# Pairwise products of an RWKV-7 layer: two 64-row products, each head in its half of the array, in place of one 128-row product with zero-filled columns

## The chip, the core and the metric

The kernel runs on one core of a Trainium2 chip. The metric is the device time of one execution in microseconds; the time before is the median of three runs. The profile is of a single execution, taken by the hardware profiler.

## What is computed

The model is a two-layer trunk on 1024 positions of width 1024. Layer 0 is a latent attention (MLA) mixer, layer 1 an RWKV-7 mixer; each has four heads of attention to a memory of 256 rows, a SiLU gate and an output projection. The change lies in layer 1, whose 24 heads of width 64 carry a state through this recurrence:

```
def step(state, inp):
    r_t, w_t, k_t, v_t, kk_t, a_t = inp
    sa = einsum('bhvk,bhk->bhv', state, -kk_t)
    state = (state * w_t[:, :, None, :]
             + sa[..., None] * (kk_t * a_t)[:, :, None, :]
             + v_t[..., None] * k_t[:, :, None, :])
    return state, einsum('bhvk,bhk->bhv', state, r_t)
```

The kernel does not step through positions. It cuts the sequence into chunks of 64 positions. Within a chunk, the products of all pairs of positions (the decayed keys against the decayed queries, one 64x64 block for each kind of pair) are made at once by a matrix multiplication and masked to the causal triangle; a triangular system is inverted, and only the state between chunks is carried in order.

## The kernel before

All work is float32. The large projections split each operand into a rounded part and a remainder and add three products (`mm3`, L160 to L162), with weights streamed from memory, rounded on ScalarE (L152) and subtracted on VectorE (L153). Other products take plain float32; each of those stands twice in the trace, as two weight loads and two passes of the moving operand.

Layer 1 works on 24 *items*: 12 pairs of heads, each for the first and then the second half of the sequence. A tile of 128 partitions holds one pair, head 0 in rows 0 to 63 and head 1 in rows 64 to 127. An item goes through five stages, `project`, `prep`, `invert`, `scan` and `norm`. In each step of the outer loop five successive items are in the five stages, and generators give their code in turn (`interleave`). The framework then places the instructions on each engine when the program is built, so the order on an engine is neither that of one stage nor quite that of the generators. Each engine executes its instructions in that order.

The change is in `prep`. An item there has eight chunks `c`, and these names:

- `BK[i][:, j, :]`, 128 partitions x 128: for a chunk, 64 columns of one kind of key and 64 of the other. It is the stationary operand.
- `AR[:, c, :]`, 128 partitions x 256: four blocks of 64 columns, two kinds (`j`) for head 0 and head 1 (`h`). The rows of head 0 are filled only in the blocks of head 0, and the rows of head 1 only in those of head 1 (L1050, L1051); the rest is zero. It is the moving operand, and the scan uses it too (L1214, L1224).
- `a_tile()`: a tile of one PSUM bank, from a pool of two. The same pool serves other products of `prep`, the memory heads and a norm.
- `AM[i]`: the masked products of two chunks, 128 x 2 x 256, read by the scan (L1212, L1225), by the DMAs to `sysd` (L1103) and by ScalarE (L1106). `am` is the mask.

Before, each chunk is one product (L1085) over all 128 rows with all 256 columns: the zeros keep the two heads apart. Two chunks fill a bank, and one VectorE multiplication by the mask (L1087) moves the bank to `AM[i]`. That is eight products, four banks and four multiplications for an item.

Two other places of layer 1 matter to the argument. `invert` has four products over 32 rows alone for each item (L1171), and eight transposes into 32 columns (L1148). The scan is a chain through the chunks: L1212 and L1214 into a bank, `gm` (L1216), L1218, `SAV` (L1219), L1221, the new state (L1233).

Of the kernel before, what the change touches and what calls it, by code (L numbers as in the profile page):

```python
# [18 lines left out]
ALU = mybir.AluOpType  # L19
# [4 lines left out]
P = 128  # L24
# [47 lines left out]
class Build:  # L72
# [903 lines left out]
    def prep(self, d, env):  # L976

        p, r, k, v, AR = (d[x] for x in ("p", "r", "k", "v", "AR"))
        twa = d["twa"]
        rmask, am, a_tile = (env[x] for x in ("rmask", "am", "a_tile"))  # L980
        nc = self.nc
        mm = nc.tensor.matmul
        V, G, ACT = nc.vector, nc.gpsimd, nc.scalar
# [7 lines left out]
        for j, (t, bias) in enumerate(((sig, PW0), (a, PA0))):  # L991
            ps = a_tile()
# [8 lines left out]
        ps = a_tile()  # L1001
# [6 lines left out]
        ps = a_tile()  # L1008
# [19 lines left out]
        f = self.smp.tile([P, 16], F32, tag="f", name=self.name("f"))  # L1028
# [9 lines left out]
        ps = a_tile()  # L1038
# [5 lines left out]
        BK = [self.g([P, 4, P], s="BK") for _ in range(2)]  # L1044
        SAV, BKT, AM = [], [], []
        V.tensor_mul(Dx[:], kk[:], Dx[:])
        V.tensor_mul(L[:], r[:], L[:])
        for hd in range(2):
            rows, c0 = slice(hd * 64, hd * 64 + 64), hd * 64
# [10 lines left out]
        ps = a_tile()  # L1060
# [9 lines left out]
        for i in range(2):  # L1070
            yield
            ps = a_tile()
# [4 lines left out]

        yield

        for i in range(4):  # L1080
            yield
            ps = a_tile()
            for j in range(2):
                c = 2 * i + j
                mm(ps[:, j * 256 : j * 256 + 256], BK[c // 4][:, c % 4, :], AR[:, c, :], start=True, stop=True)  # L1085
            AM.append(self.g([P, 2, 256], s="AM"))
            V.tensor_tensor(  # L1087
                out=AM[i][:], in0=ps[:].rearrange("p (c f) -> p c f", f=256),
                in1=am.unsqueeze(1).broadcast_to([P, 2, 256]), op=ALU.mult,
            )  # L1090

        yield

# [282 lines left out]
```

## Time and profile before

| | |
|---|---|
| three runs | 2515.22, 2519.84, 2521.16 us; median 2519.84 |
| the profiled execution | 2510.56 us, its span 2508.8 us |
| TensorE busy (PE) | 2420.2 us, 96% |
| VectorE busy (DVE) | 1936.4 us, 77% |
| ScalarE busy (ACT) | 1375.7 us, 55% |
| mean granted TensorE clock | 0.996 |
| layer 1's items, products L1085 | from 1043.8 to 2351.3 us |

PE rows are matrix passes, PEld rows the loads of their weights; a load normally runs beside the pass ahead of it. A pass is pipelined and its printed duration contains that pipeline, so the printed durations of neighbours overlap: how much array time a pass takes is read from start to start. A row of the timeline has the start, the duration, the engine, the line, the operation, the tiles (output<-inputs), then rows*columns of the array that are in use, the moving operand, and how many instructions of that kind follow one another. "32*128" is thus a weight tile over 32 rows of the array.

### The profile page before, as it was taken

How to read it: one execution, taken by the hardware profiler on the slowest of the kernel's cores; microseconds unless marked ns; L12 is line 12 of the kernel's file. 1: busy time of each engine (PE TensorE's matmuls, PEld its weight loads, DVE VectorE, ACT ScalarE, POOL GpSimd, SP SyncE). 2: the span in 40 equal slices, each digit the busy share in tenths (PEclk: the TensorE clock that was granted, in tenths of full speed). 3: DMA queues.
4: the chain of work that ended last, by engine and by line, in shares of the span. 5: the costliest groups of instructions: out<-in, count | busy, mean ns of one | idle time of the engine just before them, and what ended most of it. 6: DMA issues, size and time to landing. Idle time of an engine off the chain costs nothing.

```text
span 2508.8 us, 39875 instructions
## 1 busy us (share of the span) xinstructions
PE 2420.2 (96%) x13298; PEld 1996.1 (80%) x13298; DVE 1936.4 (77%) x5750; ACT 1375.7 (55%) x2973; POOL 55.1 (2%) x158
## 2 busy tenths in 40 slices
PE   8899999999999999999999999999999999999997
PEld 6698888888888778877778777777777777788785
DVE  7756455877787766698888888888888898786975
ACT  6445345554555334565665666666666665654542
POOL 0000000000000100000000000000000000000000
PEclk9999999999999999999999999999999999999998
DMA  5352222111112443422122222322222123222332
GB/s 178 111 171 85 76 80 74 51 56 54 49 64 68 159 168 136 143 78 76 58 73 79 80 79 78 100 82 77 79 81 80 62 84 118 87 94 98 118 137 70
DMA packets 165982, 231.45 MB, mean 92 GB/s; under 512 B 46096, under 2 KB 67984, under 8 KB 165776
## 3 DMA queue, kind: packets, MB, share of 16 engines
q1 hardware_dynamic: 165776, 228.90, 27.7%
q8 instruction: 105, 1.72, 0.3%
q14 instruction: 101, 0.83, 0.1%
HBM read 187.66 MB, written 37.49 MB: 90 GB/s over the span
## 4 chain that ended last, share of the span: by engine, by line
PE 75%; DVE 15%; ACT 6%; issue 3%; DMA 2%; SPq 0%; DVEq 0%; ACTq 0%
PE mm L160 15%; PE mm L161 15%; PE mm L162 15%; PE a L1085 3%; PE c L1218 2%; DVE tmp L1136 2%; PE pt L724 2%; DVE U L1140 2%; PE c L1221 1%; PE y L1225 1%; PE po L160 1%; PE po L161 1%; PE y L1224 1%; DVE wl L153 1%; PE po L162 1%
## 5 line engine op out<-in xcount | busy, mean ns | idle before, releaser
L152 ACT CAST wh<-wr 128x512 fp32r<-128x512 f32 (+3 forms) x500 | 299.0, 600 | 436.0 <-PE mm L161 381.0
L153 DVE TENSOR_TENSOR wl<-wr,wh 128x512 fp32r<-128x512 f32 (+3 forms) x500 | 329.6, 661 | 132.3 <-ACT wh L152 113.0
L160 PE MATMUL mm<-xnh,wh 128*128 128x512 f32 x912 | 373.9, 410 | 0.8 <-DVE qml L134 0.6
L161 PE MATMUL mm<-xnl,wh 128*128 128x512 f32 x912 | 371.2, 407 | 0.0
L162 PE MATMUL mm<-xnh,wl 128*128 128x512 f32 x912 | 369.7, 406 | 0.0
L160 PE MATMUL mm<-yh,wh 128*128 128x512 f32 x492 | 198.9, 404 | 4.3 <-DVE xr L389 4.1
L162 PE MATMUL mm<-yh,wl 128*128 128x512 f32 x492 | 196.8, 400 | 0.0
L160 PEld LDWEIGHTS mm<-xnh,wh 128*128 128x128 f32 x912 | 172.1, 189 | 30.5 <-issue 2.6
L161 PE MATMUL mm<-yl,wh 128*128 128x512 f32 x492 | 195.5, 397 | 0.0
L161 PEld LDWEIGHTS mm<-xnl,wh 128*128 128x128 f32 x912 | 172.3, 189 | 27.2 <-issue 1.4
L162 PEld LDWEIGHTS mm<-xnh,wl 128*128 128x128 f32 x912 | 172.1, 189 | 27.3 <-issue 1.0
L160 PE MATMUL mm<-xh,wh 128*128 128x512 f32 x416 | 165.2, 398 | 7.6 <-ACT xh L438 7.6
L161 PE MATMUL mm<-xl,wh 128*128 128x512 f32 x416 | 164.9, 396 | 0.6 <-DVE xl L439 0.6
L1140 DVE TENSOR_TENSOR U<-U,tmp 128x60 f32<-128x60 f32 (+24 forms) x744 | 155.9, 210 | 12.3 <-PE b L1171 0.5
L1136 DVE TENSOR_TENSOR tmp<-As,U 128x60 f32<-128x60 f32 (+24 forms) x744 | 155.6, 209 | 12.1
L162 PE MATMUL mm<-xh,wl 128*128 128x512 f32 x416 | 164.3, 395 | 0.0
L1232 ACT ACTIVATE sc<-S,f 128x128 f32<-128x128 f32 x168 | 67.4, 401 | 169.5 <-DVE S L1233 155.9
L302 ACT ACTIVATE p<-b,sm 128x512 f32<-128x512 f32 (+2 forms) x144 | 82.8, 579 | 107.3 <-DVE sm L299 82.2
L389 DVE TENSOR_TENSOR xr<-mm,xr 128x512 f32<-128x512 f32 x123 | 84.5, 688 | 67.1 <-PE mm L162 65.2
L160 PEld LDWEIGHTS mm<-yh,wh 128*128 128x128 f32 x492 | 92.7, 188 | 22.6 <-DVE xr L389 3.5
L297 DVE TENSOR_REDUCE sm<-b 128x1 f32<-128x256 f32 (+1 forms) x176 | 90.3, 527 | 24.8 <-PE b L686 10.1
L162 PEld LDWEIGHTS mm<-yh,wl 128*128 128x128 f32 x492 | 92.7, 188 | 17.0 <-issue 0.2
(361 smaller groups left out, 5968.8 us busy)
## 6 DMA issues: line engine op xcount, KB each, us to landing
wr<-in_wu_dram SPq DMA_DIRECT2D x292, 256.0 KB, 2.7
wr<-in_wo_dram SPq DMA_DIRECT2D x122, 256.0 KB, 2.6
yr<-y SPq DMA_DIRECT2D x60, 256.0 KB, 3.8
As<-sysd SPq DMA_DIRECT2D x24, 512.0 KB, 4.3
y<-y SPq DMA_DIRECT2D x32, 256.0 KB, 2.0
y<-sg SPq DMA_DIRECT2D x32, 256.0 KB, 2.0
g<-u SPq DMA_DIRECT2D x24, 256.0 KB, 2.3
gt<-g SPq DMA_DIRECT2D x24, 256.0 KB, 2.8
```

The costliest lines, as they stand in the source:

```text
L152: nc.scalar.copy(hi[:, :n], raw[:, :n])
L153: nc.vector.tensor_sub(lo[:, :n], raw[:, :n], hi[:, :n].bitcast(F32))
L160: mm(ps, a[0], b[0], start=start, stop=False)
L161: mm(ps, a[0], b[1], start=False, stop=False)
L162: mm(ps, a[1], b[0], start=False, stop=stop)
L297: nc.vector.tensor_reduce(sm[:, i : i + 1], ps[:, :own], AX.X, ALU.max, negate=True)
L302: nc.scalar.activation(p[:, :own], ps[:, :own], AF.Exp, bias=sm[:, 0:1], accum_out=sm[:, 2 + i : 3 + i])
L389: nc.vector.tensor_add(xs[m][:], ps[:], xs[m][:])
L1085: mm(ps[:, j * 256 : j * 256 + 256], BK[c // 4][:, c % 4, :], AR[:, c, :], start=True, stop=True)
L1136: E.tensor_tensor(out=tmp[:, 0:u, 0:n], in0=As[:, 0:u, u : u + 1].broadcast_to([P, u, n]), in1=U[:, u : u + 1, i0:8].broadcast_to([P, u, n ...
L1140: E.tensor_tensor(out=U[:, 0:u, i0:8], in0=U[:, 0:u, i0:8], in1=tmp[:, 0:u, 0:n], op=ALU.add)
L1232: ACT.activation(sc[:], cur, AF.Copy, scale=fc)
```

## The change

Each chunk becomes two products, one for each head. A product takes the head's 64 rows of `BK` and `AR` alone, and of `AR` only that head's two blocks of 64 columns, so that 128 columns move and no zeros. The two heads use different halves of the array's rows and write into two banks, four chunks to a bank. The bank pair is then multiplied by the mask in four pieces, each of two chunks and one head, into the same places of `AM` as before.

```
-        for i in range(4):
+        by_head = lambda t, hd: t.rearrange("p (j h t) -> p j h t", j=2, h=2)[:, :, hd, :]
+        for g in range(2):
             yield
-            ps = a_tile()
-            for j in range(2):
-                c = 2 * i + j
-                mm(ps[:, j * 256 : j * 256 + 256], BK[c // 4][:, c % 4, :], AR[:, c, :], start=True, stop=True)
-            AM.append(self.g([P, 2, 256], s="AM"))
-            V.tensor_tensor(
-                out=AM[i][:], in0=ps[:].rearrange("p (c f) -> p c f", f=256),
-                in1=am.unsqueeze(1).broadcast_to([P, 2, 256]), op=ALU.mult,
-            )
+
+            pss = [a_tile(), a_tile()]
+            for j in range(4):
+                for hd in range(2):
+                    rows = slice(hd * 64, hd * 64 + 64)
+                    mm(
+                        pss[hd][:, j * P : j * P + P].rearrange("p (j t) -> p j t", j=2), BK[g][rows, j, :],
+                        by_head(AR[rows, 4 * g + j, :], hd), start=True, stop=True,
+                    )
+            yield
+            for i in range(2):
+                AM.append(self.g([P, 2, 256], s="AM"))
+                for hd in range(2):
+                    V.tensor_tensor(
+                        out=AM[-1][:].rearrange("p c (j h t) -> p c j h t", j=2, h=2)[:, :, :, hd, :],
+                        in0=pss[hd][:, i * 256 : i * 256 + 256].rearrange("p (c j t) -> p c j t", c=2, j=2),
+                        in1=by_head(am, hd).unsqueeze(1).broadcast_to([P, 2, 2, 64]), op=ALU.mult,
+                    )
```

Lines behind this place have numbers higher by ten: L1212 becomes L1222. The new products are L1088, the new multiplications L1096.

On TensorE, the first group of chunks of the third item stood like this before (`a` is the bank; between the products stand pieces of the scan of an earlier item):

```order
L1085 MATMUL a_12173<-AR_10127,BK_12011 128x256
L1221 MATMUL c_12052<-SAV_11120,BKT_11157 128x128
L1225 MATMUL y_11918<-SAV_11120,AM_11263 128x128
L1085 MATMUL a_12173<-AR_10127,BK_12011 128x256
L1085 MATMUL a_12178<-AR_10127,BK_12011 128x256
L1212 MATMUL c_12081<-SAV_11120,AM_11263 128x128
L1214 MATMUL c_12081<-S_2585_11916,AR_10125 128x128
L1224 MATMUL y_11918<-S_2585_11916,AR_10125 128x128
L1085 MATMUL a_12178<-AR_10127,BK_12011 128x256
L1218 MATMUL c_12086<-gm_12084,XT_10128 128x128
```

All of these use the array's 128 rows. Now the same place of TensorE's order reads as follows, where `a_12197` is the bank of head 0 (rows 0 to 63) and `a_12198` that of head 1 (rows 64 to 127):

```order
L1088 MATMUL a_12197<-AR_10127,BK_12035 128x128 x2
L1231 MATMUL c_12076<-SAV_11120,BKT_11157 128x128
L1235 MATMUL y_11942<-SAV_11120,AM_11268 128x128
L1088 MATMUL a_12198<-AR_10127,BK_12035 128x128 x2
L1088 MATMUL a_12197<-AR_10127,BK_12035 128x128
L1088 MATMUL a_12198<-AR_10127,BK_12035 128x128
L1222 MATMUL c_12105<-SAV_11120,AM_11268 128x128
L1224 MATMUL c_12105<-S_2585_11940,AR_10125 128x128
L1234 MATMUL y_11942<-S_2585_11940,AR_10125 128x128
L1088 MATMUL a_12197<-AR_10127,BK_12035 128x128
L1088 MATMUL a_12198<-AR_10127,BK_12035 128x128
L1228 MATMUL c_12110<-gm_12108,XT_10128 128x128
```

Four products of 256 columns became eight of 128, in three blocks with 128-row products ahead of and behind each. Over the whole program there are 384 products L1088 in 128 such blocks: 16 blocks have one product, 46 two, 29 three, 19 four, 11 five or six, 7 eight.

On VectorE, the multiplications by the mask of that group stood among the steps of the inversion (`tmp`, `U`) and of the scan like this:

```order
L1087 TENSOR_TENSOR AM_12176<-a_12173,cst 128x512
L1136 TENSOR_TENSOR tmp_11829<-As_11826,U_11828 128x12x5
L1216 TENSOR_TENSOR gm_12161<-c_12158,cst 128x128
L1140 TENSOR_TENSOR U_11828<-U_11828,tmp_11829 128x12x5
L1087 TENSOR_TENSOR AM_12181<-a_12178,cst 128x512
```

Now there are four, each of half the width, and the last one that reads a bank stands ten rows behind the first:

```order
L1096 TENSOR_TENSOR AM_12207<-a_12197,cst 128x4x64
L1146 TENSOR_TENSOR tmp_11853<-As_11850,U_11852 128x12x5
L1096 TENSOR_TENSOR AM_12207<-a_12198,cst 128x4x64
L1150 TENSOR_TENSOR U_11852<-U_11852,tmp_11853 128x12x5
L1226 TENSOR_TENSOR gm_12185<-c_12182,cst 128x128
L1146 TENSOR_TENSOR tmp_11853<-As_11850,U_11852 128x11x6
L1096 TENSOR_TENSOR AM_12210<-a_12197,cst 128x4x64
L1150 TENSOR_TENSOR U_11852<-U_11852,tmp_11853 128x11x6
L1229 COPY SAV_11124<-c_12187 64x128
L1146 TENSOR_TENSOR tmp_11853<-As_11850,U_11852 128x10x6
L1096 TENSOR_TENSOR AM_12210<-a_12198,cst 128x4x64
```

The bank of head 0 is free after the third, that of head 1 after the fourth. The rest of the program keeps its instructions; some of them stand a few places earlier or later.

## The prediction

> **What bounds the kernel.** I read the page first, for the shares of the span and the chain that ended last. Its rows are the busy time and share of each engine, and the chain's shares by engine.
>
> ```profile
> span 2508.8 us, 39875 instructions
> ...
> PE 2420.2 (96%) x13298; PEld 1996.1 (80%) x13298; DVE 1936.4 (77%) x5750; ACT 1375.7 (55%) x2973; POOL 55.1 (2%) x158
> ...
> PE 75%; DVE 15%; ACT 6%; issue 3%; DMA 2%; SPq 0%; DVEq 0%; ACTq 0%
> ```
>
> TensorE is the bound. Next I read the stretch in which the changed products lie, 1040 to 2360 us, as one window, and the chain by line for that stretch.
>
> ```profile
> 1040.00:2360.00 1320.00, 1280.79 (x7098) 1040.32 (x7097) 1114.80 (x3866) 814.74 (x1784) 22.84 (x44) 1.00 0.26 83
> by line: PE mm L160 11.5%; PE mm L162 11.1%; PE mm L161 11.1%; PE a L1085 6.0%; DVE tmp L1136 3.1%; issue 3.0%; DVE U L1140 2.9%; PE c L1218 2.8%; PE c L1221 2.6%; PE y L1225 2.3%; PE y L1224 2.1%; PE c L1212 2.0%; PE c L1214 1.9%; ACT yT L
> ```
>
> After the length come PE, PEld, DVE and ACT busy. In this stretch PE is busy for 1280.8 of 1320 us and DVE for 84%, at the full granted clock (1.00). The products L1085 alone are 6.0% of the chain there, 79 us. Array time given or taken at this place therefore shows almost fully in the end.
>
> **The products.** What they take now is read from the groups by form (the count, then busy time and mean) and from start to start in the timeline.
>
> ```profile
> L1085 PE MATMUL a<-AR,BK 128*128 128x256 f32 x384 | 101.6, 382 | 0.0
> L1087 DVE TENSOR_TENSOR AM<-a,cst 128x512 f32<-128x512 f32 x96 | 65.2, 681 | 1.8 <-PE a L1085 0.8 <-PE y L1224 0.4
> L738 DVE TENSOR_TENSOR y<-po,gt 128x256 f32<-128x256 f32 x48 | 20.1, 419 | 3.3 <-PE po L162 3.1
> ...
> 1434.08 1.46 PE L1085 MATMUL a<-AR,BK 128*128 128x256 f32 x6
> ...
> 1438.51 0.38 PE L1212 MATMUL c<-SAV,AM 128*128 128x128 f32 x2
> 1438.73 0.39 PE L1214 MATMUL c<-S,AR 128*128 128x128 f32 x2
> ```
>
> Six passes L1085 last 1.46 us and one 0.38, so a pass of 256 columns takes (1.46 - 0.38) / 5 = 0.216 us. Two passes of 128 columns take 0.22 (1438.51 to 1438.73), 0.110 each. The 384 passes are 82.9 us, and nearly all of it was the 79 us of the chain.
>
> The change makes 768 passes of 128 columns from them. If the halves of the array take turns, that is 768 x 0.110 = 84.5 us: nothing is gained, because the zeros that are left out were columns, and the columns of the two heads add up to as many. Only if a pass of head 0 runs beside one of head 1 is there a gain. How much depends on the order: I let a pass start beside the one ahead of it only when that one is in the other half, and not before it. Going block by block through the built order, a block of two alternating products then takes three slots for its four passes, and the 128 blocks take 576 slots, 63.4 us. No row of this trace shows two halves at work together. The ends are therefore 63.4 and 84.5; no row is nearer to either, and I take the middle, 74.0: 8.9 us less than now.
>
> **The switch of the array's rows.** The kernel already has products over fewer rows, L1171 over 32. The PE timeline at two of these places, and the weight loads at the first:
>
> ```profile
> 1399.93 0.39 PE L162 MATMUL mm<-mpth,mvs 128*128 128x512 f32 x1
> 1400.16 0.40 PE L993 MATMUL a<-twa,w2h 128*128 128x512 f32 x1
> 1400.48 1.15 PE L1171 MATMUL b<-X,inv 32*128 32x128 f32 x8
> 1401.57 0.51 PE L994 MATMUL a<-twa,w2l 128*128 128x512 f32 x1
> 1401.91 0.39 PE L993 MATMUL a<-twa,w2h 128*128 128x512 f32 x1
> ...
> 1668.12 0.39 PE L162 MATMUL mm<-xnh,wl 128*128 128x512 f32 x1
> 1668.44 1.15 PE L1171 MATMUL b<-X,inv 32*128 32x128 f32 x8
> 1669.52 0.50 PE L160 MATMUL mm<-xnh,wh 128*128 128x512 f32 x1
> 1669.86 0.40 PE L161 MATMUL mm<-xnl,wh 128*128 128x512 f32 x1
> ...
> 1399.93 0.19 PEld L993 LDWEIGHTS a<-twa,w2h 128*128 128x128 f32 x1
> 1400.48 0.96 PEld L1171 LDWEIGHTS b<-X,inv 32*128 32x128 f32 x8 [0.36 <-DVE U L1140]
> 1401.57 0.19 PEld L994 LDWEIGHTS a<-twa,w2l 128*128 128x128 f32 x1
> 1401.67 0.19 PEld L993 LDWEIGHTS a<-twa,w2h 128*128 128x128 f32 x1
> ```
>
> A load usually starts with the pass ahead of its own: that of L993 starts at 1399.93, its pass at 1400.16. The first load of L1171 does not: it starts at 1400.48, together with its own pass and 0.32 us after the start of L993, whose array time is only 0.23. The same happens on leaving: the load of L994 starts with its pass at 1401.57. From L993 at 1400.16 to the second 512-column pass behind it at 1401.91 are 1.75 us, and the array time in between is 0.23 + 8 x 0.11 + 0.23 = 1.34. The block costs 0.41 us beyond its passes. The second place gives 1669.86 - 1668.12 - 1.34 = 0.40. The waiting row names VectorE's `U` as releaser on the way in; on the way out there is no such name, and both ways are as long, so I read this as the price of the switch itself, 0.20 each way: the array empties, then a load stands bare. Fewer columns, in contrast, cost nothing:
>
> ```profile
> 1447.33 0.39 PE L162 MATMUL mm<-xnh,wl 128*128 128x512 f32 x1
> 1447.55 0.60 PE L1148 MATMUL b<-cst,U 128*32 128x128 f32 x4
> 1447.99 0.39 PE L1212 MATMUL c<-SAV,AM 128*128 128x128 f32 x2
> ```
>
> Four passes into 32 columns take 0.44 us from start to start with no gap on either side. The change puts 64-row products into 128 blocks, each with 128-row products on both sides, and before it had none: 128 x 0.40 = 51.2 us on TensorE. The ends are 0 (the L1148 row, a narrow tile that costs nothing) and 51.2 (the L1171 rows, where rows are fewer, as here); I take the nearer, 51.2.
>
> The Trainium skill, "TensorEngine Tiling (Array Packing)", section Tiling Modes, says of this that "Changing tiling mode (not just tile) drains the TensorE". It speaks against the change: by it a switch to 64 rows must drain as the 32-row blocks do in this trace, and going from one half to the other inside a block must not. Its next point, that tiles load weights and multiply in parallel, would put the products at 63.4 us and the sum of both terms at +31.7 instead of +42.3; no run here shows that part yet.
>
> **VectorE.** 96 multiplications of 512 columns (65.2 us) become 192 of 256 from a bank; L738 is such an operation, at 0.419. That is 80.4 us, 15.2 more. VectorE has 16% free in this stretch and is 15% of the page's chain, so I put 0.15 x 15.2 = 2.3 us on the path; the ends are 0 and 15.2.
>
> **The banks.** Both banks of the pool are now taken together, and the second group's first product waits for the third multiplication of the first. Before, this wait was small, in the answer on L1085:
>
> ```profile
> its engine sat idle before it (us, times) until:
>   ACT BKT L1076: 1.3, 7
>   DVE AM L1087: 0.5, 2
> ```
>
> Its cover is the projection and scan products that stand between the groups, in the third item 17 of them, about 3 us, against 4 x 0.419 = 1.7 us of multiplications. I take 1 us for the program; the ends are 0 and, if that cover is gone for all 24 items, 24 x 1.7 = 40. ScalarE's copies, the DMAs of `AM` and the scan's reads are the same in number and bytes; the copies and DMAs feed the inversion one step later and have a step's time as cover.
>
> **The sum.** TensorE: 51.2 - 8.9 = +42.3 us. Between 0.75 (PE's share of the whole chain) and 0.95 (79 of L1085's 82.9) reach the end; some blocks stand where TensorE waits for the scan anyway, and I take 0.9: +38.1. With 2.3 and 1.0 it is +41.4. The profiled execution took 2510.56 us and would take 2552; it lies 9.3 us under the median of the three runs, and on the median, 2519.84, the forecast is 2561 us, 1.6% slower. About 0.3%, 7.6 us, is what a measurement of this kernel can tell from no change.
>
> **The rivals.** (a) *Faster: the halves overlap and the switch to 64 rows is free*, as for L1148. Then TensorE has 63.4 - 82.9 = -19.5; with 0.9 and the 3.3 of the other terms that is -14, 2506 us. It decides if a block's switch costs less than about 0.12 us ((19.5 x 0.9 - 3.3) / (128 x 0.9)). Against it stand the L1171 rows. Chance 0.10. (b) *It does nothing for the array*: no overlap, free switch, 84.5 - 82.9 = +1.6, with the rest +5: 2525 us. Chance 0.07. (c) *VectorE binds*: all 15.2 us fall on the path, +54, 2574 us. For it speaks its 84% in the stretch; against it, that slower products leave it more room. Chance 0.06. (d) *The banks bind*: TensorE stands before the second group in most items; with half of the 40 us it is +60, 2580 us, with all +80. The 0.5 us of now and the 17 products between speak against it. Chance 0.07.
>
> **How the numbers follow.** My forecast, the switch paid, has 0.70. Its own range goes from overlap at the low share of the chain, 31.7 x 0.75 + 3.3 = +27, to turns at the high share, 52.8 x 0.95 + 3.3 = +53: 2547 to 2573 us. The range of 8 in 10 reaches from 2522, which takes in (b), to 2585, which takes in (c) and the first half of (d); it leaves out (a) and the rest of (d). Faster by over 0.3% is (a), 0.10; within 0.3% is (b), 0.07; slower is the rest, 0.83.
>
> **What the next profile would show.** The switch: the first load of an L1088 block starting with its own pass, and 0.40 us more than the passes from the 128-row pass ahead to the second one behind. The overlap: passes L1088 of the two banks starting in pairs, a block of eight products taking about 1.0 us (9 x 0.110) rather than 1.8 (16 x 0.110). The multiplications: 0.42 us each. The banks: L1088 waiting for AM for more than a few us. I am wrong if a block of 64-row products follows a 128-row pass without a gap; then the time is below 2530. I am also wrong if going from one half to the other drains too, which would show as 0.2 us between passes and put the time above 2590.

## The result

The changed kernel takes 2531.35 us (median of four runs, 2530.25 to 2533.18) against 2517.66 for the kernel before (four runs, 2515.22 to 2521.16). The ratio is 1.0051, with a 95% interval of 1.0035 to 1.0067: 13 us slower by the ratio, where 41 were forecast. The direction was right, the size three times too large; the time lies below the 2547 to 2573 us that the forecast gave for its own mechanism.

The page of the profile after, the rows that answer to those of before:

```profile
span 2531.3 us, 40731 instructions
...
PE 2448.4 (97%) x13682; PEld 2004.6 (79%) x13682; DVE 1942.1 (77%) x5846; ACT 1374.6 (54%) x2973; POOL 55.4 (2%) x158
...
PE 76%; DVE 13%; ACT 6%; issue 2%; DMA 2%; SPq 0%; DVEq 0%; ACTq 0%
```

The groups of the new products and multiplications, with their idle time and what ended it:

```profile
L1088 PE MATMUL a<-AR,BK 64*128 64x128 f32 x768 | 91.0, 302 | 0.0
L1096 DVE TENSOR_TENSOR AM<-a,cst 128x256 f32<-128x256 f32 x192 | 76.9, 418 | 7.7 <-PE a L1088 6.8
L1088 PEld LDWEIGHTS a<-AR,BK 64*128 64x128 f32 x768 | 66.3, 187 | 21.0 <-issue 4.1 <-ACT BKT L1076 1.5 <-DVE SAV L1229 1.5
```

TensorE is still the bound and is 28 us busier. The multiplications cost what L738 said (0.418). TensorE's loads do not wait for the multiplications: among all the releasers of L1088, of which the row shows three, AM does not appear. The timeline of TensorE at the first block, eight products and so sixteen passes:

```profile
1046.56 0.39 PE L162 MATMUL mm<-yh,wl 128*128 128x512 f32 x1
1046.88 1.16 PE L1088 MATMUL a<-AR,BK 64*128 64x128 f32 x16
1047.97 0.50 PE L160 MATMUL mm<-yh,wh 128*128 128x512 f32 x1
1048.31 0.39 PE L161 MATMUL mm<-yl,wh 128*128 128x512 f32 x1
```

From 1046.56 to 1048.31 are 1.75 us. The two 512-column passes take 0.23 each, the switch 0.39 in all, and 0.90 is left for sixteen passes that would take 1.79 in turn: they run in eight pairs. The trace's starts of single passes show it: the first two are 6 ns apart, then 0.207 us pass with the bare loads, then a pair starts every 0.112 us. Two smaller blocks, in the scan of the third item:

```profile
1126.57 0.93 PE L1088 MATMUL a<-AR,BK 64*128 64x128 f32 x8
1127.43 0.49 PE L1222 MATMUL c<-SAV,AM 128*128 128x128 f32 x2
1127.76 0.39 PE L1224 MATMUL c<-S,AR 128*128 128x128 f32 x2
1127.98 0.39 PE L1234 MATMUL y<-S,AR 128*128 128x128 f32 x2
1128.30 0.49 PE L1088 MATMUL a<-AR,BK 64*128 64x128 f32 x4
1128.72 0.49 PE L1228 MATMUL c<-gm,XT 128*128 128x128 f32 x2
```

The block at 1128.30 has two products. From L1234 at 1127.98 to L1228 at 1128.72 are 0.74 us; two passes L1234 take 0.22 of it, and the first pass of L1228 still waits for its bare load. Over all 128 blocks the medians are 0.195 us for the way in, 0.193 for the way out, and for the passes 0.23 (blocks of two products), 0.45 to 0.46 (three and four) and 0.90 (eight). (14 of the 46 blocks of two start no pair and take 0.45; the order shown ahead of the prediction has such a block, with both products in one bank and so in one half.) Over 128 rows, two products take 0.45, four 0.89 and eight 1.79. So with 0.39 for the switch a block of two loses, one of four breaks even, and only long ones gain; 91 of the 128 blocks have three products or fewer.

One sum serves below. For each block I take the time from the start of the pass ahead to the start of the second pass behind, less the array time of those two, and add up the blocks; waits inside are contained, those of the first product too. Before, this is 87 us, after, 112: TensorE spends 25 us more. Each such sum is from one profiled execution, each time and ratio from several.

### The profile page after: what moved, and what is told of

Its sections match the earlier page's. It is cut to its first block, busy times and chain, and to the rows that moved or that the text cites. A ratio compares the mean times of both kernels' runs of the same rounds, so it can differ in the third digit from the quotient of the medians.

```text
span 2531.3 us, 40731 instructions
## 1 busy us (share of the span) xinstructions
PE 2448.4 (97%) x13682; PEld 2004.6 (79%) x13682; DVE 1942.1 (77%) x5846; ACT 1374.6 (54%) x2973; POOL 55.4 (2%) x158
## 4 chain that ended last, share of the span: by engine, by line
PE 76%; DVE 13%; ACT 6%; issue 2%; DMA 2%; SPq 0%; DVEq 0%; ACTq 0%
PE mm L160 16%; PE mm L162 15%; PE mm L161 15%; PE a L1088 3%; PE c L1228 2%; PE c L1231 2%; PE pt L724 2%; PE y L1235 1%; PE c L1222 1%; DVE wl L153 1%; PE po L160 1%; PE po L161 1%; DVE tmp L1146 1%; PE y L1234 1%; DVE U L1150 1%
```

## The experiments

The theory: the switches cost TensorE 0.39 us a block, the overlap gives passes back, and most of either reaches the end. The rival: TensorE's part is absorbed by waits, and the loss comes from the narrow multiplications and from holding both banks.

### No switch and no overlap: the heads apart, over 128 rows

The two operands of `mm` change, the rest of the call (`...`) stays:

```
-  ... BK[g][rows, j, :],
-  by_head(AR[rows, 4 * g + j, :], hd), ...
+  ... BK[g][:, j, :],
+  by_head(AR[:, 4 * g + j, :], hd), ...
```

> The products of the changed kernel, one for each head into its own bank, but over all 128 rows (the other head's rows are zero in these columns): no row switch and no overlap, while the bank pairs and the eight narrow multiplications on VectorE stay. Theory (the loss is the 128 row switches on TensorE, about 0.39 us each, against a gain from the overlap): TensorE has 768 passes of 0.110 = 84.5 us instead of 82.9, so the time is that of the kernel before plus 1 to 5 us, ratio 1.000 to 1.002. Rival (the switches are absorbed by waits, and the loss comes from VectorE's narrow multiplications and from holding both banks): the same loss as the changed kernel or more, plus 10 to 16 us, ratio 1.004 to 1.006.

Measured: 2515.5 against 2518.3 us, ratio 0.9989 (0.9979 to 0.9998). The kernel stands in exactly the changed kernel's order on TensorE, VectorE and ScalarE, with the same multiplications and banks, and it is 3 us faster than the kernel before, not 10 to 16 slower. The rival falls. The theory's plus 1 to 5 us is missed too, a little on the other side: TensorE's blocks take 93 us, 6 more than before, so the narrow multiplications, the banks and the new order together cost nothing here.

### The switch without the overlap: both heads on one half

```
-  ... BK[g][rows, j, :],
-  by_head(AR[rows, 4 * g + j, :], hd), ...
+  ... BK[g][0:64, j, :],
+  by_head(AR[0:64, 4 * g + j, :], hd), ...
```

This kernel leaves out head 1's products: rows 0 to 63 hold zeros in the columns of head 1.

> The changed kernel with both heads' products put on rows 0 to 63, so that head 1's products use the rows of head 0 and its masked products come out as zeros; on every engine the instructions stand in exactly the order of the changed kernel. All 128 blocks switch, and no pass has a partner in the other half. Theory (switches cost TensorE 0.39 us each block, overlap gives back 28.7 us of passes, some eight tenths of either reach the end): TensorE has about 141 us in these blocks against 112 in the changed kernel, so 20 to 27 us slower than it and 34 to 40 slower than before, ratio 1.013 to 1.016. Rival (what TensorE saves or loses here is mostly absorbed by waits of the scan): within 8 us of the changed kernel, ratio 1.004 to 1.008.

Measured: ratio 1.0162 (1.0146 to 1.0179), 2560.0 us, 41 slower than before and 28 slower than the change; the theory's upper ends were 40 and 27. With it there are three kernels of the same order on these engines. Their first block, first in this kernel, then in the one over 128 rows:

```profile
1047.82 0.39 PE L162 MATMUL mm<-yh,wl 128*128 128x512 f32 x1
1048.14 2.05 PE L1088 MATMUL a<-AR,BK 64*128 64x128 f32 x16
1050.12 0.50 PE L160 MATMUL mm<-yh,wh 128*128 128x512 f32 x1
1050.45 0.39 PE L161 MATMUL mm<-yl,wh 128*128 128x512 f32 x1
```

```profile
1049.99 0.39 PE L162 MATMUL mm<-yh,wl 128*128 128x512 f32 x1
1050.22 1.95 PE L1088 MATMUL a<-AR,BK 128*128 128x128 f32 x16
1051.92 0.48 PE L160 MATMUL mm<-yh,wh 128*128 128x512 f32 x1
1052.23 0.40 PE L161 MATMUL mm<-yl,wh 128*128 128x512 f32 x1
```

Between the 512-column passes at the ends lie 2.63 us on one half (1047.82 to 1050.45), 2.24 over 128 rows, and 1.75 with both halves. The switch is the 0.39 between the first two, the overlap the 0.88 between the first and the last. In the whole program:

| | TensorE in the blocks | ratio to before | against the row above |
|---|---|---|---|
| over 128 rows | 93 us | 0.9989 | |
| one half: switch alone | 137 us | 1.0162 | +44 us for +44 on TensorE |
| both halves: switch and overlap (the change) | 112 us | 1.0051 | -28 us for -25 on TensorE |

The last column is the difference of the ratios times 2518 us. Within 5 to 6 us, which the intervals of the ratios allow, what TensorE gains or loses at this place comes out whole at the end, and the change loses because 128 switches (44 us) cost more than the overlap returns (28).

The granted clock of the runs bears on these differences. Within one kernel, a run whose mean granted clock is 0.001 lower is 2.1 us longer (slope over 102 runs of these kernels). The mean is 0.9929 for the kernel over 128 rows, 0.9918 on one half, 0.9938 for the change and 0.9936 for the kernel before. Brought to one clock with this slope, which is an estimate, the steps of the table are 41 us for 44 on TensorE and 24 for 25, and from the first row to the last 18 for 19: a little over nine tenths each time. The change then stays 14 us slower than the kernel before.

### One block for each group

The eight products of a group are traced at high priority, each behind the one ahead, and the first waits until both banks are free. That gives 48 blocks of alternating products.

In short (`...` marks what is left out; `freed` is the instruction that frees the other bank):

```
+            with self.tc.high_priority():
+                last = None
+                for j in range(4):
+                    for hd in range(2):
...
+                        with self.tc.issue_after(last) if last else nullcontext():
+                            last = mm(
...
+                        if j == 0 and hd == 0:
+                            self.tc.add_manual_dep(
+                                last, freed.name, ...
```

> The changed kernel with the eight products of a group held together, alternating between the heads: 48 blocks of 64-row products instead of 128, nothing else changed in what is computed. Theory: TensorE spends 48 x (8 x 0.112 + 0.39) = 61.7 us in place of 82.9 before and about 107 in the changed kernel; with 0.55 to 0.75 of that reaching the end, 11 to 16 us faster than the kernel before, less some 2 us of VectorE: ratio 0.994 to 0.997. Rival (VectorE and the banks cause the loss): no better than the changed kernel, ratio 1.004 to 1.007.

Measured: 2510.0 us, ratio 0.9965 (0.9953 to 0.9977), 9 us faster than before and 21 faster than the change. The theory's range holds it, at its weak end: TensorE's blocks take 65 us, 22 less than before, and the time is 9 us less. The order of the instructions changed too; what it costs is measured below.

### The same blocks without pairs

```
-  for j in range(4):
-      for hd in range(2):
+  for hd in range(2):
+      for j in range(4):
```

> As the kernel with 48 blocks, but in each block all four products of head 0 stand ahead of the four of head 1, so that few passes find a partner in the other half. Theory: a block takes 1.6 to 1.8 us and 0.39 for its switches instead of 0.9 and 0.39, so TensorE has 96 to 105 us, 13 to 22 more than before: ratio 1.003 to 1.008, and 16 to 25 us slower than with the pairs. If the overlap is worth nothing to the end, both kernels with 48 blocks take the same time.

Measured: ratio 1.0037 (1.0024 to 1.0050), 2528.9 us, 19 slower than with the pairs, as expected. The two kernels do not stand in the same order (2500 of TensorE's 13682 passes are others at their place), so not all of the 19 us need be the overlap; the next experiment keeps the order. The blocks take less than I expected, 91 us in all: a block's passes last 1.45 us, 13 slots of 0.112 rather than 16, so TensorE finds some partners even with four products of one half ahead of four of the other.

### The same order over 128 rows

The kernel with 48 blocks, with the operands of the first experiment.

> The kernel with 48 blocks, in exactly its order on every engine, but with the products over all 128 rows: no switch and no overlap. Theory: TensorE has 86 us of passes and a few of waits, about 92 instead of 65, 27 more; with 0.75 of that at the end, 20 us slower than the kernel with 48 blocks, ratio 1.004 to 1.006, which would also say that this order costs some 10 us against the order of the kernel before. Rival (this order costs nothing and time saved on TensorE is only worth four tenths): 8 to 12 us slower than it, ratio 0.999 to 1.001.

Measured: 2528.4 us, ratio 1.0037 (1.0023 to 1.0050), 18 us slower than the kernel with 48 blocks, whose order it has on every engine. The theory said 20; the rival's 8 to 12 falls. TensorE has 91 us in the blocks instead of 65, so 0.7 of its gain reaches the end (0.6 brought to one clock as above). And this kernel does the work of the first experiment with the same time in the blocks, 91 against 93 us, but takes 12 us more (10 at one clock): the wait for both banks is inside the blocks, so holding products together at high priority costs that much outside them, in the order of everything else. Where the rest, 8 us, goes is seen in the waits of TensorE's loads for the scan. First with the switch and the pairs, then over 128 rows:

```profile
PEld c L1239 <- DVE gm L1237: 23.7, 59, 1.0
PEld c L1242 <- DVE SAV L1240: 19.1, 58, 2.1
PEld c L1233 <- DVE S L1254: 9.1, 33, 0.6
```

```profile
PEld c L1239 <- DVE gm L1237: 14.9, 46, 0.8
PEld c L1242 <- DVE SAV L1240: 14.7, 51, 2.0
PEld c L1233 <- DVE S L1254: 7.5, 31, 0.6
```

Each row has the total, the count and the longest in us. When TensorE is through earlier, its loads wait 15 us longer for VectorE's steps of the scan (51.9 against 37.1). A waiting load can still stand beside a running pass, so not all of that is lost: by the two pages, span less busy time, PE is idle for 93 us against 86.

### 79 blocks

The edit for 48 blocks, with `high_priority(20)`.

> The changed kernel with the alternating products held together less strictly: 79 blocks of 64-row products, between the 128 of the changed kernel and the 48 of the kernel with one block for each group. Theory: TensorE has 79 x 0.39 us of switches and about 45 us of passes, some 80 in all with waits, 7 less than before; the time lies between the two, 2512 to 2518 us, ratio 0.998 to 1.000. Rival (not the number of blocks but the order that comes with strict holding decides): not between them, at or below the 48 blocks (ratio 0.996 or less) or at the changed kernel (1.004 or more).

Measured: ratio 1.0048 (1.0034 to 1.0061). The theory's place between the two kernels is missed and the rival holds: TensorE's blocks take 82 us, 5 less than before, and yet the time is 12 us more (7 at one clock; it has the lowest mean, 0.9912). So a count of blocks alone does not predict the time between kernels of different order. That the order outweighs the blocks here, directly or through the clock, is not shown: no run has this order over 128 rows.

### The switch of the kernel before, at L1171

The kernel before has 24 such blocks of its own. Here their products run over 128 rows, with zeros from GpSimd:

```
+  X1 = self.g([P, 16, 32], s="X1")
+  for t in (X1[32:64], X1[64:128], inv[96:128]):
+      G.memset(t, 0.0)
...
-  A21[:, 4 * g4 : 4 * g4 + 4, :]
+  inv[:, 4 * g4 : 4 * g4 + 4, :]
```

> The kernel before, unchanged in the pairwise products, but the 24 blocks of 32-row products L1171 run over 128 rows, with zeros written into the other rows by GpSimd: the switch price alone. Theory: 24 x 0.39 = 9.4 us less on TensorE, of which 0.55 to 0.75 reach the end: 5 to 7 us faster, ratio 0.997 to 0.998. Rival (switches cost the array but are absorbed by waits of the chain around them): within 2 us of the kernel before, ratio 0.999 to 1.001.

Measured: ratio 1.0011 (1.0002 to 1.0019), no gain. The control keeps the zeros and the buffer, and the 32 rows:

> The control to the kernel before without the L1171 switch: GpSimd writes the same zeros and the same buffer is held, but L1171 still runs over 32 rows; on every engine the instructions stand in exactly the order of that kernel. Theory that a switch costs the end as much as the array: this one is 5 to 7 us slower than the kernel without the switch, ratio 1.003 to 1.004 against the kernel before, and the zeros and the buffer ate the gain there. Rival (at L1171 the switch is absorbed, because the next step waits for ScalarE anyway): both take the same time within 2 us, ratio 1.000 to 1.002.

Measured: ratio 1.0028 (1.0017 to 1.0040). The two have the same order, in which the 24 blocks became 33; the switch makes 0.0017 between them, 4 us (3 at one clock), for 9 us on TensorE (38 and 29 us in these blocks). The zeros, the longer-held buffer and the changed order together cost 7 us and ate the gain. The two intervals overlap, so this pair is weak: the 4 us lie between the theory's 5 to 7 and the rival's 0 to 2 and rule out neither. A part of the switch, half or less, seems to reach the end at this place; the products behind it (L1185, here L1187) wait 19.3 us for ScalarE without the switch and 13.1 with it.

## Why the prediction was wrong in size

**The bound and the switch: right.** 0.40 us for each block, read from L1171, was forecast for 64 rows; 0.39 was measured. 128 blocks make 50 us against 51.2, and 44 us at the end in kernels of equal order. The Trainium skill, "TensorEngine Tiling (Array Packing)", section Tiling Modes, is borne out in both points on the switch that I cited: changing the mode from 128 to 64 rows drains the array, and changing the tile from one half to the other does not. On the way in, the first load starts 0.09 us after the array time of the pass ahead is over (1046.56 + 0.23, then 1046.88); inside the block a pair starts every 0.112 us. One reading beside it was too wide: "fewer columns cost nothing" holds for the transposes L1148, but the 24 blocks L1185 of the kernel before, also 128*32, end with a bare load, 0.20 us each (last pass at 1403.58, the next pass and its load at 1403.78). Why the two differ is not shown; the forecast rested on the other end, the L1171 rows.

**The products: the term that was mis-sized.** I took 74.0 us, the middle between turns (84.5) and my overlap (63.4). The passes take 57.4 us (from the first pass's data to the last's, summed over the blocks), below even my best case. Two steps failed. The larger is the middle: because no row showed two halves at work together, I discounted half of the overlap, 10.6 us (74.0 less 63.4), and all of it came: blocks of eight take 0.90 us, not 1.79. The other, 6.0 us (63.4 less 57.4), is the rule that a pass starts "not before" the one ahead of it. Each product is two passes, and I let head 1's first pass wait for head 0's second. In the trace the first passes of the two products start 6 ns apart, so an alternating block of an even number n of products takes n slots, not n + 1. Together that is 16.6 us too much on TensorE, 15 with the 0.9. What no run had shown before, that the halves load and multiply in parallel, is now seen: two loads and two passes fit into 0.112 us.

**VectorE and the banks: wrong in sign, but small.** I took +3.3 us. The kernel over 128 rows, with all of this and 3.3 us more passes (86.2 against 82.9), is 2.8 us faster than before; without these passes, at 0.9, the rest is worth about -5.7, so 9 us of the error lie here. VectorE's own time was about right (15.2 us more was forecast; 76.9 against 65.2 are 11.7), and the multiplications L1096 have no piece in the chain that ended last. The interval of the 2.8 us reaches 2.4 us to either side. How much of the gain is order, and how much finer pieces, stays open: the order moved with the change, and another order moved the time by 10 to 12 us.

**The share that reaches the end.** 0.9 was forecast. In kernels of equal order 44 of 44 and 28 of 25 us came out around the change, and so 16 of 19 between the kernel over 128 rows and the change. At one clock it is 41, 24 and 18, so 0.9 was about right for the change. By the times as measured 3 to 4 us remain, which are only what the other terms leave over; the interval of the result is 4 us to either side. A gain from 91 to 65 us on TensorE came out to 0.7 only.

41.4 less 15 for the overlap and 9 for VectorE, banks and order gives 17, less 1 for the switch (51.2 against 50) 16; with the remainder it is the 13 that were measured. All these errors went the same way, so none hid another, and the right direction rests on the switch, the largest term.

**The rivals.** Free switches (a, b): no, the load of the first pass starts with it at 1046.88, as at L1171, and the switch alone costs 44 us. VectorE or the banks as the bound (c, d): no, the first experiment.

## What to carry over

Packing two 64-row products into the array halves the time of their passes at best (0.90 us against 1.79 for eight), but each block pays a fixed price at both ends, so count the blocks in the built order before counting passes: here a block broke even at four products. Interleaving that was free with 128-row products is what made the change lose; held in blocks of eight, the same products made the fastest kernel of this study, 0.35% under the kernel before. To weigh a term, compare kernels whose instructions stand in the same order, and look at the granted clock of the runs: with equal work and equal time in the blocks, another order moved this kernel by 10 to 12 us, as much as the effects in question.

## What was not expected of the hardware

The two halves do more than overlap as written: a pass of one half overtakes a waiting pass of the other that stands ahead of it in the program. In the first of the 48 blocks, the load that waits for the second product's semaphore is the third to start over 128 rows, and the second, 6 ns behind the first, with both halves. So TensorE does not execute strictly in the order in which its instructions stand, as was said of each engine ahead of the prediction. The overtaking has a limit. Four products on one half ahead of four on the other took 13 slots, alternating ones 8. The weight loads keep up: two loads for the two halves and two passes fit into 0.112 us, where one load and one pass over 128 rows take 0.110.
